# Regrouping the f32 matmuls of a two-layer trunk: transposes of a head in one run, weighted values ahead of the next scores, numerators two at a time

## The chip, the cores and the metric

The kernel runs on one core of one Trainium2 chip. The metric is the device time of one execution in microseconds (us), the median of several runs. TensorE is called PE, VectorE DVE, ScalarE ACT, SyncE SP.

## The reference, cut to what matters

The input x has 512 tokens (S) of 2048 features. It goes through two layers, each with a normalisation in front, a modulation by a conditioning vector c, a gated branch and a normalised residual.

The first layer is an mLSTM with 8 heads. In the kernel's form each head has a 512 x 512 lower-triangular weight matrix over tokens (score of key and query, times exponential gate weights), and the numerator is this matrix applied to the values:

```
s = einsum(q, k) * w_intra
num = w_inter * (q C) + s v        # 512 value columns a head
h = num / max(|den|, exp(-m))
y = sigmoid(o) * rmsnorm(h) * silu(z)
```

The second layer is attention with 16 heads of 128 features, a bias by clipped distance, and chunks of 64 tokens; with 512 tokens all earlier chunks are in reach:

```
s = einsum(q, k) * scale + bias
p = softmax(s)
o = p v                            # 128 columns a head
y = o * silu(z)
```

## The kernel before, in words

Everything is float32. A large matmul is not done in plain f32: both operands are split into a high and a low part of the type fp32r (helper `split`, L181: a cast on ACT, L182, and a subtraction on DVE, L183), and three matmuls add up high x high, high x low and low x high (`mm3`, L226, through `mm`, L223 and L224). Such a triple is the unit of most of the work. Some small matmuls stay in plain f32: one call of `mm` on f32 tiles, which PE runs as two instructions, and the transposes of L1070, one instruction each.

Weights come from memory in pieces of up to 128 x 1024 (`wpiece`, L188), in one fixed order, through SP's DMA queue (L200). Each piece is split into high and low (tiles wh and wl); for projections by a seven-product scheme (`proj_s`, L266) sums of weight blocks (ws, L207 to L209) are made on DVE and split as well (wsh, wsl).

PSUM has eight banks, one tile of 128 x 512 f32 each. Five belong to projections (`newp`, psP), three to all else (`newa`, psA). A scheduler orders each engine's instructions by data dependence, by the order in the program and by priorities; `tc.high_priority(AHEAD)` lets evacuations go first. A tile of a pool of n buffers waits until the tile n places earlier has been read.

mLSTM, one pass of the loop at L632 per head: the projections q, k; the values (ps_v) with the score tiles woven in (`scores`, L601); the gates o and z; the sum of weights ps_d; then the numerators, L732 to L744. For each of four column tiles i of the head's values, ps_n takes nine fp32r matmuls (j = 0, 1, 2: 512, 384 and 256 columns, the weights being triangular) and one f32 matmul of 128 columns (L737). ACT squares it (L740), DVE multiplies it into the gate (L741) and adds up the squares (L744). ps_q sums these over partitions (L746).

Attention, the loop at L1097: pass h projects queries and gate of head h (`queries`, L1026, one `proj_s` of four pieces). Between its pieces stand the steps of the two heads before, given as a table {1: turn, 2: mid, 3: end}. A head's life is: `weights` (L1045) for row tiles 0 and 3 in mid, and for 1 and 2 in end, of the pass after its projection: scores ps_s, with tile 0 in f32 (kt and zq) and the others by triples; the bias and the maximum in one DVE instruction (L1058), the exponential on ACT (L1059), the reciprocal and the multiplication by it on DVE (L1060, L1061). Then `flipped` (L1064) transposes the 128 x 128 blocks of the row tiles (triangular: ten of them) into ps_t and splits them into pt: column tiles 0 and 1 at the end of the pass (L1126), tiles 2 and 3 in turn (L1101). Each column tile has a bank of its own. Finally `mixed` (L1086) in mid multiplies by the values: ps_o, nine fp32r matmuls and one f32 (vt), then the gate (L1093) and a store (y2c, L1094). In mid the scores of head h-1 stand ahead of the weighted values of head h-2, and the fetch of the next k (`fetch_k`, kt, L1016) stands behind both.

Behind the attention the last projection (b_w_out, ps_y) reads y2c; the attention's last steps are woven into its first matmuls.

Of the kernel before, what the change touches and what calls it, by code (L numbers as in the profile page):

```python
# [9 lines left out]
F32 = mybir.dt.float32  # L10
F32R = mybir.dt.float32r
AF = mybir.ActivationFunctionType
ALU = mybir.AluOpType
AX = mybir.AxisListType

P = 128
D = 2048
S = 512
KT = D // P
NH = 8  # L20
# [7 lines left out]
BH = 16  # L28
# [4 lines left out]
AHEAD = 300  # L33
# [93 lines left out]
GHEAD = CBIAS + 32  # L127
# [5 lines left out]
def hybrid_trunk(ctx, tc, xT, xN, c, adaT, cols, wst, wg, ext, kc, out):  # L133
    nc = tc.nc
# [8 lines left out]
    def pool(name, bufs=1, **kw):  # L143
        return tc.tile_pool(name=name, bufs=bufs, reuse_waits="tile", **kw)
# [31 lines left out]
    def col(i):  # L176
        return cl[:, i : i + 1]
# [3 lines left out]
    def split(hi, lo, src):  # L181
        nc.scalar.copy(hi, src)  # L182
        nc.vector.tensor_tensor(lo, src, hi.bitcast(F32), op=ALU.subtract)  # L183
# [39 lines left out]
    def mm(ps, a, b, start, stop):  # L223
        nc.tensor.matmul(ps, a, b, start=start, stop=stop)  # L224

    def mm3(ps, ah, al, bh, bl, start, stop):  # L226
        mm(ps, ah, bh, start, False)
        mm(ps, ah, bl, False, False)
        mm(ps, al, bh, False, stop)
# [121 lines left out]
    def newp(name):  # L351
        return psP.tile([P, S], F32, tag="p", name=name)

    def newa(name):
        return psA.tile([P, S], F32, tag="a", name=name)
# [8 lines left out]
    tp = phA.enter_context(pool("t1", bufs=3, side="right"))  # L364
# [42 lines left out]
    for q in range(4):  # L407
        t = sp.tile([P, 4, S], F32, name=f"xt{q}")
# [8 lines left out]
    for i in range(4):  # L417
        ps = newp(f"ps_c{i}")
# [3 lines left out]
    pss = newa("ps_x")  # L422
# [5 lines left out]
    for q in range(4):  # L428
        pair = []
        for i in range(2):  # L430
            sq = xp.tile([P, 2, S], F32, tag="x", name=f"xsq{q}_{i}")
# [28 lines left out]
    for k0, k1 in BLOCKS:  # L460
# [10 lines left out]
        for i, acc in enumerate(later):  # L471
            ps = newa(f"ps_l{i}_{k0}")
# [128 lines left out]
    def scores(h, j, qk, pr, nm, nmd, tot):  # L601

        n = S - P * j
        t0 = min(P * j, 256)
        ps = newa(f"ps_s{h}_{j}")
        for kk in range(2):
            q, k = qk[kk], qk[2 + kk]
            s = slice(j * P, (j + 1) * P)
            mm3(ps[:, : S - t0], k[:, 0, s], k[:, 1, s], q[:, 0, t0:], q[:, 1, t0:], kk == 0, kk == 1)
        psn = ps[:, P * j - t0 : S - t0]  # L610
        e = tp.tile([P, S], F32, tag="t", name=f"e{h}_{j}")
        a = aT[:, j, h : h + 1]
        nc.scalar.activation(e[:, 0:P], nmd[:, j, :], AF.Exp, bias=a)
        if n > P:
            nc.scalar.activation(e[:, P:n], nm[:, P * (j + 1) :], AF.Exp, bias=a)
        if j < 3:
            with tc.high_priority(AHEAD):
                nc.vector.scalar_tensor_tensor(e[:, :n], psn, DK**-0.5, e[:, :n], op0=ALU.mult, op1=ALU.mult)
            t = hp.tile([P, 2, n], F32R, tag=f"p{j}", name=f"p{h}_{j}")
            split(t[:, 0, :], t[:, 1, :], e[:, :n])  # L620
        else:
            t = hp.tile([P, n], F32, tag=f"p{j}", name=f"p{h}_{j}")
            nc.vector.scalar_tensor_tensor(t, psn, DK**-0.5, e[:, :n], op0=ALU.mult, op1=ALU.mult)
        pr.append(t)
        if j == 0:
            tot.append(e)
        else:
            nc.vector.tensor_tensor(
                tot[0][:, P * j :], tot[0][:, P * j :], e[:, :n] if j < 3 else t, op=ALU.add
            )  # L630

    for h in range(NH):  # L632
# [3 lines left out]
        if h == 0:  # L636
            so = oz[:4]
        qk = []
        for i in range(4):
            if h > HALF:  # L640
                if i % 2 == 0:
                    zs = pair((i // 2) * (V0 // 2) + h * DK, f"zq{h}_{i}")
                ps = zs[i % 2]
            elif h < 2:
                ps = (lead, qk1)[h][i]
            else:
                ps = newp(f"ps_qk{h}_{i}")
# [24 lines left out]
        pr, tot = [], []  # L672
        at = {8 + 2 * j: lambda j=j: scores(h, j, qk, pr, nm, nmd, tot) for j in range(4)} if h else {}
# [10 lines left out]
        v = []  # L684
        for m in range(4):
            with tc.high_priority(AHEAD):
                if m < 3:
                    t = hp.tile([P, 2, S], F32R, tag="qk", name=f"v{h}_{m}", bufs=4)
                    split(t[:, 0, :], t[:, 1, :], pv[m])
                else:  # L690
                    t = hp.tile([P, S], F32, tag="nm", name=f"v{h}_{m}")
# [4 lines left out]
        if h:  # L696
            so = []
        for i in range(4):
            if h >= HALF:
                f = HEAD_PAIRS if h > HALF else RAMP[i]  # L700
# [5 lines left out]
            elif h:  # L706
                ps = newp(f"ps_o{h}_{i}")
# [4 lines left out]
        for i in range(4):  # L712
            if h >= HALF:
                break
            if h:
                ps = newp(f"ps_z{h}_{i}")
                proj_a("a_w_in", h1, ps)
            else:
                ps = oz[4 + i]
# [9 lines left out]
        nc.vector.tensor_tensor(dd, dd, em, op=ALU.max)  # L729
        nc.scalar.activation(dd, dd, AF.Square, scale=EPS**0.5)  # L730
        sqs = hp.tile([P, S], F32, tag="nmd", name=f"sqs{h}")
        for i in range(4):  # L732
            d = slice(i * P, (i + 1) * P)
            ps = newa(f"ps_n{h}_{i}")
            for j in range(3):
                mm3(ps[:, P * j :], v[j][:, 0, d], v[j][:, 1, d], pr[j][:, 0, :], pr[j][:, 1, :], j == 0, False)
            mm(ps[:, 384:], v[3][:, d], pr[3], False, True)  # L737
            with tc.high_priority(AHEAD):
                sq = sqs if i == 0 else tp.tile([P, S], F32, tag="t", name=f"sq{h}_{i}")
                nc.scalar.activation(sq, ps, AF.Square)  # L740
                nc.vector.scalar_tensor_tensor(so[i], ps, col(GHEAD + 4 * h + i), so[i], op0=ALU.mult, op1=ALU.mult)  # L741
            if i:
                with tc.high_priority(AHEAD if h == NH - 1 else 0):
                    nc.vector.tensor_tensor(sqs, sqs, sq, op=ALU.add)  # L744
        ps = newa(f"ps_q{h}")
        sums(ps, sqs, f"q{h}", *((AHEAD, 80) if h == NH - 1 else ()))  # L746
        nc.vector.scalar_tensor_tensor(dd, ps, 1.0 / DV, dd, op0=ALU.mult, op1=ALU.add)
# [19 lines left out]
    tp = tst.enter_context(pool("t2", bufs=6, side="right"))  # L767
# [127 lines left out]
    def scale_steps(*ks):  # L895
        at = {k: lambda: (scale_sums(), scale_load()) for k in ks}
        return at | {k + 2: scale_load for k in ks}
# [3 lines left out]
    for pair, ms in enumerate(PAIRS):  # L901
        for g in range(1, 4):
            at = scale_steps(4, 12, 20, *([28] if g < 3 else [])) if pair == 0 else {}
            if pair == 0 and g == 3:
                at[28] = lambda: (scale_sums(), amul_cols(2, 48 + KT, GPRE + KT))
            if pair == 1 and g == 1:
                at = {2: lambda: residual(0), 4: lambda: residual(1)}
                at |= {20 + 4 * i: lambda i=i: turned(0, [i], False) for i in range(3)}
            if pair == 1 and g == 2:
                at = {2: lambda: turned(0, [3], False)}  # L910
            if pair == 1 and g == 3:
                at = {k: lambda k=k: [key_input(i, kept(i, slice(0, 2 * P)), slice(0, 2 * P)) for i in range(k // 2 - 1, k // 2 + 1)] for k in range(2, 32, 4)}
# [60 lines left out]
    for i in range(KT // 2):  # L973
        z = zp.tile([P, 4, 256], F32, tag="z", name=f"zk{i}")
        ready = len(hs)
        at = {2: input_sums} if ready < KT // 2 else {}
# [8 lines left out]
    for g in range(2, 4):  # L985
        n = -(-ATT_PAIRS // 2)
# [22 lines left out]
    at = ast.enter_context(pool("att"))  # L1009
# [51 lines left out]
            nc.vector.tensor_scalar(s, s, r, None, op0=ALU.mult)  # L1061
            pr[i] = s

    def flipped(h, pr, js):  # L1064
        pts = []
        for j in js:
            n = S - P * j
            ps = newa(f"ps_t{h}_{j}")
            for i in range(j, 4):
                nc.tensor.transpose(ps[:, P * (i - j) : P * (i - j + 1)], pr[i][:, P * j : P * (j + 1)], ident)  # L1070
            with tc.high_priority(AHEAD):
                if j < 3:
                    t = at.tile([P, 2, n], F32R, tag=f"pt{j}", name=f"pt{h}_{j}")
                    split(t[:, 0, :], t[:, 1, :], ps[:, :n])
                else:
                    t = at.tile([P, n], F32, tag=f"pt{j}", name=f"pt{h}_{j}")
                    nc.scalar.copy(t, ps[:, :n])
            pts.append(t)
        return pts

# [5 lines left out]
    def mixed(h, pts, v, sz):  # L1086
        ps = newa(f"ps_o{h}")
        for j in range(3):
            d = slice(P * j, P * (j + 1))
            mm3(ps[:, P * j :], v[:, 0, d], v[:, 1, d], pts[j][:, 0, :], pts[j][:, 1, :], j == 0, False)  # L1090
        mm(ps[:, 384:], vt[h][:, 384:], pts[3], False, True)
        with tc.high_priority(AHEAD):
            nc.vector.tensor_tensor(sz, ps, sz, op=ALU.mult)  # L1093
        nc.sync.dma_start(y2c[h // 2][:, h % 2, :], sz)  # L1094

    qs, pts, prs, vs, szs = {}, {}, {}, {}, {}
    for h in range(BH + 2):  # L1097

        def turn():
            if h > 1:  # L1100
                pts[h - 2] += flipped(h - 2, prs.pop(h - 2), (2, 3))  # L1101
                vs[h - 2] = split_v(h - 2)

        def mid():
            if 0 < h <= BH:
                weights(h - 1, (0, 3), *qs[h - 1])
            if h > 1:
                mixed(h - 2, pts.pop(h - 2), vs.pop(h - 2), szs.pop(h - 2))
            if 0 < h < BH:
                fetch_k(h)  # L1110
            if h < BH:
                fetch_v(h)

        def end():
            if 0 < h <= BH:
                weights(h - 1, (1, 2), *qs[h - 1])
                prs[h - 1] = qs.pop(h - 1)[0]

        if h < BH:
            qs[h], szs[h] = queries(h, {1: turn, 2: mid, 3: end})  # L1120
        else:
            turn()
            mid()
            end()
        if 0 < h <= BH:
            pts[h - 1] = flipped(h - 1, prs[h - 1], (0, 1))  # L1126
    ast.close()


# [1 line left out]
    op = ost.enter_context(pool("op", bufs=KT))  # L1131
# [64 lines left out]
    for g in range(4):  # L1196
        if g:
            spare[0] = rp
        for pair in [range(4)] if g < 3 else PAIRS:
            ps = [newp(f"ps_y1_{g}_{m}") for m in pair]  # L1200
            at = {4: lambda: finish(0), 6: lambda: finish(1)} if pair == PAIRS[1] else {}
# [65 lines left out]
```

## Time and profile before

| | |
|---|---|
| median of 3 runs | 2799.73 us (2799.65 to 2801.61) |
| profiled execution | 2801.9 us |
| its span, first to last instruction | 2800.1 us |
| granted TensorE clock, mean | 0.998 |
| DMA | 527.09 MB, mean 188 GB/s |
| transposes ps_t | 160, median record 272 ns |
| f32 block of ps_o (vt) | 32 instructions, median record 275 ns |

A row of the timeline has the start in us, the length, the engine, the line, the operation and its tiles (output, then inputs), the shape, and the number of equal instructions merged; matmuls are pipelined, so the lengths of neighbours overlap, and the distance between starts is what PE spends. A row of the windows view has the stretch, its length, and the busy time of PE, weight loads (PEld), DVE, ACT and GpSimd with their instruction counts, then the granted clock, the DMA share and GB/s. A row of the waits view has who waited for whom, the sum in us, how often, and the longest.

### The profile page before, as it was taken

What the parts mean: (1) busy time and instruction counts of PE and PEld (TensorE: products, weight loads), DVE (VectorE), ACT (ScalarE), POOL (GpSimd) and SP (SyncE); (2) the same over time, 40 slices, a digit from 0 to 9 for tenths busy, and PEclk for the clock granted to TensorE, in tenths of its full rate; (3) what the DMA queues carried; (4) which work ended last, traced back from release to release, by engine and by line L of the source; (5) the groups of instructions that cost most, each with busy time, mean ns of one, the idle gap of its engine ahead of it and who ended that gap; (6) DMA issues with size and microseconds to landing.
All of it is one profiled execution on the core that took longest, in us unless ns stands there. A gap on an engine that the chain in (4) does not pass through costs nothing.

```text
span 2800.1 us, 42223 instructions
## 1 busy us (share of the span) xinstructions
PE 2767.4 (99%) x15959; PEld 2440.4 (87%) x15959; DVE 2157.3 (77%) x3788; ACT 1370.5 (49%) x2032; POOL 0.2 (0%) x4
## 2 busy tenths in 40 slices
PE   7999999999999999999999999999999999999998
PEld 5887888888998989989999788888999899999887
DVE  7986979769786876867867677567986788989667
ACT  4234524234454554545545344568534466666523
POOL 0000000000000000000000000000000000000000
PEclk9999999999999999999999999999999999999999
DMA  8875697865232332323324889879535544444687
GB/s 296 305 255 180 219 320 249 305 215 180 93 112 94 102 113 91 113 91 106 115 89 140 274 294 303 264 255 298 177 136 174 173 128 125 123 129 128 218 299 250
DMA packets 182999, 527.09 MB, mean 188 GB/s; under 512 B 19669, under 2 KB 38133, under 8 KB 182153
## 3 DMA queue, kind: packets, MB, share of 16 engines
q1 hardware_dynamic: 182794, 524.38, 56.6%
q8 instruction: 125, 2.05, 0.3%
q14 instruction: 80, 0.66, 0.1%
HBM read 490.69 MB, written 38.85 MB: 189 GB/s over the span
## 4 chain that ended last, share of the span: by engine, by line
PE 85%; DVE 6%; DMA 5%; issue 2%; ACT 2%; SPq 0%; DVEq 0%; ACTq 0%
PE ps_y L224 15%; PE ps_v L224 12%; PE ps_azo L224 5%; PE ps_kv L224 4%; PE ps_o L224 4%; PE ps_bzo L224 3%; PE ps_az L224 3%; PE ps_cz L224 3%; PE ps_dz L224 3%; PE ps_qk L224 3%; PE ps_z L224 3%; PE ps_czo L224 3%; PE ps_dzo L224 3%; PE ps_s L224 2%; PE ps_n L224 2%
## 5 line engine op out<-in xcount | busy, mean ns | idle before, releaser
L182 ACT CAST wh<-wr 128x1024 fp32r<-128x1024 f32 (+3 forms) x586 | 585.3, 1000 | 707.4 <-PE ps_y L224 151.8
L183 DVE TENSOR_TENSOR wl<-wr,wh 128x1024 fp32r<-128x1024 f32 (+3 forms) x586 | 679.1, 1161 | 284.6 <-ACT wh L182 283.5
L224 PE MATMUL ps_y<-wh,y 128*128 128x512 f32 x1536 | 478.1, 391 | 2.4 <-ACT y L182 1.8
L224 PEld LDWEIGHTS ps_y<-wh,y 128*128 128x128 f32 x1536 | 288.1, 188 | 64.8 <-ACT y L182 3.0
L182 ACT CAST wsh<-ws 128x384 fp32r<-128x384 f32 (+1 forms) x261 | 163.3, 626 | 361.0 <-PE ps_az L224 126.1
L224 PE MATMUL ps_v<-wh,h 128*128 128x512 f32 x1024 | 322.7, 391 | 0.4 <-DVE zq L318 0.4
L224 PE MATMUL ps_y<-wl,y 128*128 128x512 f32 x768 | 299.5, 390 | 0.0
L183 DVE TENSOR_TENSOR wsl<-ws,wsh 128x384 fp32r<-128x384 f32 (+1 forms) x261 | 181.8, 697 | 121.2 <-ACT wsh L182 119.4
L224 PEld LDWEIGHTS ps_v<-wh,h 128*128 128x128 f32 x1024 | 192.5, 188 | 40.9 <-DVE zq L318 0.9
L224 PE MATMUL ps_v<-wl,h 128*128 128x512 f32 x512 | 199.8, 390 | 0.0
L224 PEld LDWEIGHTS ps_y<-wl,y 128*128 128x128 f32 x768 | 144.3, 188 | 29.5 <-DVE wl L183 0.3
L224 PE MATMUL ps_kv<-wh,hkv 128*128 128x512 f32 x512 | 159.4, 391 | 0.0
L207 DVE TENSOR_TENSOR ws<-wr 128x256 f32<-128x256 f32 (+1 forms) x261 | 132.2, 516 | 33.4 <-DMA wr<-in_wst 31.3
L382 DVE CUSTOM_DVE_ANT_0 ada<-ada,scB,mod 128x1024 f32<-128x1024 f32 x96 | 123.0, 1282 | 16.4 <-DMA ada<-in_adaT 15.4
L382 DVE CUSTOM_DVE_ANT_0 ada<-ada,scB,cl 128x1024 f32<-128x1024 f32 x96 | 122.9, 1281 | 13.0 <-DMA ada<-in_adaT 12.8
L224 PEld LDWEIGHTS ps_kv<-wh,hkv 128*128 128x128 f32 x512 | 96.2, 188 | 19.7
L224 PEld LDWEIGHTS ps_v<-wl,h 128*128 128x128 f32 x512 | 96.3, 188 | 19.5 <-issue 0.9
L224 PE MATMUL ps_azo<-h,wh 128*128 128x256 f32 (+1 forms) x406 | 101.4, 332 | 1.1 <-DVE zo L318 1.1
L224 PE MATMUL ps_l<-h,wh 128*128 128x512 f32 x320 | 99.4, 393 | 0.5 <-ACT oz L475 0.5
L224 PE MATMUL ps_kv<-wl,hkv 128*128 128x512 f32 x256 | 99.9, 390 | 0.0
L224 PE MATMUL ps_czo<-h1s,wsh 128*128 128x256 f32 x468 | 89.3, 283 | 0.0
L209 DVE TENSOR_TENSOR ws<-wr 128x128 f32<-128x128 f32 (+1 forms) x261 | 85.2, 336 | 3.6
(390 smaller groups left out, 6266.0 us busy)
## 6 DMA issues: line engine op xcount, KB each, us to landing
wr<-in_wst SPq DMA_DIRECT2D x520, 512.0 KB, 3.7
ada<-in_adaT SPq DMA_DIRECT2D x224, 512.0 KB, 6.0
adq<-in_adaT SPq DMA_DIRECT2D x64, 256.0 KB, 5.7
xt<-nsc SPq DMA_DIRECT2D x48, 256.0 KB, 4.0
yr<-ysc SPq DMA_DIRECT2D x16, 512.0 KB, 4.6
wr<-in_wst SPq DMA_DIRECT2D x30, 256.0 KB
wr<-in_wst SPq DMA_DIRECT2D x16, 384.0 KB, 9.6
bsc<-in_ext SPq DMA_DIRECT2D x16, 320.0 KB, 6.5
```

Source lines behind the costliest of these rows:

```text
L182: nc.scalar.copy(hi, src)
L183: nc.vector.tensor_tensor(lo, src, hi.bitcast(F32), op=ALU.subtract)
L207: nc.vector.tensor_tensor(t[:, : 2 * w], r[:, w : 3 * w], r[:, : 2 * w], op=ALU.subtract)
L209: nc.vector.tensor_tensor(t[:, 2 * w :], r[:, 3 * w :], r[:, w : 2 * w], op=ALU.subtract)
L224: nc.tensor.matmul(ps, a, b, start=start, stop=stop)
L382: pin(nc.vector.tensor_tensor_reduce(at, at, (sc or scB)[:, j * D // 2 : (j + 1) * D // 2], 1.0, mod[:, i : i + 1] if j else col(CB + i), ...
```

## The change

Three edits. In the mLSTM the numerators are written in twos: the nine fp32r matmuls of both tiles first, then both f32 matmuls, then both evacuations. In the attention all ten transposes of a head are done in turn, one after the other, into three banks (column tile 3 shares the bank of tile 1); the call at the end of the pass is gone. In mid the weighted values of head h-2 stand ahead of the scores of head h-1.

```diff
-        for i in range(4):
-            d = slice(i * P, (i + 1) * P)
-            ps = newa(f"ps_n{h}_{i}")
-            for j in range(3):
-                mm3(ps[:, P * j :], v[j][:, 0, d], v[j][:, 1, d], pr[j][:, 0, :], pr[j][:, 1, :], j == 0, False)
-            mm(ps[:, 384:], v[3][:, d], pr[3], False, True)
...
+        for i0 in (0, 2):
+            pss = [newa(f"ps_n{h}_{i}") for i in (i0, i0 + 1)]
+            ds = [slice(i * P, (i + 1) * P) for i in (i0, i0 + 1)]
+            for ps, d in zip(pss, ds):
+                for j in range(3):
+                    mm3(ps[:, P * j :], v[j][:, 0, d], v[j][:, 1, d], pr[j][:, 0, :], pr[j][:, 1, :], j == 0, False)
+            for ps, d in zip(pss, ds):
+                mm(ps[:, 384:], v[3][:, d], pr[3], False, True)
+            for i, ps in zip((i0, i0 + 1), pss):
...
-    def flipped(h, pr, js):
-        pts = []
-        for j in js:
-            n = S - P * j
-            ps = newa(f"ps_t{h}_{j}")
+    def flipped(h, pr):
+
+        banks = [newa(f"ps_t{h}_{j}") for j in range(3)]
+        pss = [banks[0], banks[1][:, :384], banks[2][:, :256], banks[1][:, 384:]]
+        for j, ps in enumerate(pss):
             for i in range(j, 4):
                 nc.tensor.transpose(ps[:, P * (i - j) : P * (i - j + 1)], pr[i][:, P * j : P * (j + 1)], ident)
+        pts = []
+        for j, ps in enumerate(pss):
             with tc.high_priority(AHEAD):
...
         def turn():
             if h > 1:
-                pts[h - 2] += flipped(h - 2, prs.pop(h - 2), (2, 3))
+                pts[h - 2] = flipped(h - 2, prs.pop(h - 2))
                 vs[h - 2] = split_v(h - 2)
 
         def mid():
+            if h > 1:
+                mixed(h - 2, pts.pop(h - 2), vs.pop(h - 2), szs.pop(h - 2))
             if 0 < h <= BH:
                 weights(h - 1, (0, 3), *qs[h - 1])
-            if h > 1:
-                mixed(h - 2, pts.pop(h - 2), vs.pop(h - 2), szs.pop(h - 2))
...
-        if 0 < h <= BH:
-            pts[h - 1] = flipped(h - 1, prs[h - 1], (0, 1))
```

More of the change, by code (lines that the diff above doesn't have):

```diff
@@ L731, in hybrid_trunk @@
         sqs = hp.tile([P, S], F32, tag="nmd", name=f"sqs{h}")
-        for i in range(4):
-            d = slice(i * P, (i + 1) * P)
-            ps = newa(f"ps_n{h}_{i}")
-            for j in range(3):
-                mm3(ps[:, P * j :], v[j][:, 0, d], v[j][:, 1, d], pr[j][:, 0, :], pr[j][:, 1, :], j == 0, False)
-            mm(ps[:, 384:], v[3][:, d], pr[3], False, True)
[L738 to L744, printed above, removed]
+        for i0 in (0, 2):
[7 more added lines that the diff above has]
+            for i, ps in zip((i0, i0 + 1), pss):
+                with tc.high_priority(AHEAD):
+                    sq = sqs if i == 0 else tp.tile([P, S], F32, tag="t", name=f"sq{h}_{i}")
+                    nc.scalar.activation(sq, ps, AF.Square)
+                    nc.vector.scalar_tensor_tensor(so[i], ps, col(GHEAD + 4 * h + i), so[i], op0=ALU.mult, op1=ALU.mult)
+                if i:
+                    with tc.high_priority(AHEAD if h == NH - 1 else 0):
+                        nc.vector.tensor_tensor(sqs, sqs, sq, op=ALU.add)
         ps = newa(f"ps_q{h}")
@@ L1062, in weights @@
             pr[i] = s
-    def flipped(h, pr, js):
-        pts = []
-        for j in js:
-            n = S - P * j
-            ps = newa(f"ps_t{h}_{j}")
+    def flipped(h, pr):
+        banks = [newa(f"ps_t{h}_{j}") for j in range(3)]
+        pss = [banks[0], banks[1][:, :384], banks[2][:, :256], banks[1][:, 384:]]
+        for j, ps in enumerate(pss):
             for i in range(j, 4):
                 nc.tensor.transpose(ps[:, P * (i - j) : P * (i - j + 1)], pr[i][:, P * j : P * (j + 1)], ident)
+        pts = []
+        for j, ps in enumerate(pss):
             with tc.high_priority(AHEAD):
                 if j < 3:
-                    t = at.tile([P, 2, n], F32R, tag=f"pt{j}", name=f"pt{h}_{j}")
-                    split(t[:, 0, :], t[:, 1, :], ps[:, :n])
-                else:
-                    t = at.tile([P, n], F32, tag=f"pt{j}", name=f"pt{h}_{j}")
-                    nc.scalar.copy(t, ps[:, :n])
+                    t = at.tile([P, 2, S - P * j], F32R, tag=f"pt{j}", name=f"pt{h}_{j}")
+                    split(t[:, 0, :], t[:, 1, :], ps)
+                else:
+                    t = at.tile([P, P], F32, tag=f"pt{j}", name=f"pt{h}_{j}")
+                    nc.scalar.copy(t, ps)
             pts.append(t)
```

## The prediction

> **What bounds the kernel now.** I read the page first: which engine is busy, and which engine the chain that ended last runs through.
>
> ```profile
> span 2800.1 us, 42223 instructions
> PE 2767.4 (99%) x15959; PEld 2440.4 (87%) x15959; DVE 2157.3 (77%) x3788; ACT 1370.5 (49%) x2032; POOL 0.2 (0%) x4
> PE 85%; DVE 6%; DMA 5%; issue 2%; ACT 2%; SPq 0%; DVEq 0%; ACTq 0%
> ```
>
> TensorE (PE) is busy for 99% of the span, so I asked next for its busy time in the stretches that the edits touch: the numerators of one head (1509 to 1532 us, the last of eight), the attention (2255 to 2628), and four microseconds of its end.
>
> ```profile
> 1509.00:1532.00 23.00, 23.00 (x118) 19.85 (x117) 17.73 (x27) 14.63 (x22) 0.00 (x0) 1.00 0.54 176
> 2255.00:2628.00 373.00, 372.85 (x2949) 365.55 (x2949) 333.93 (x734) 245.74 (x434) 0.00 (x0) 1.00 0.45 139
> 2622.00:2626.00 4.00, 4.00 (x25) 3.29 (x23) 2.48 (x5) 2.89 (x7) 0.00 (x0) 1.00 0.98 374
> ```
>
> The columns after the stretch are its length, then PE, weight loads, DVE and ACT. PE stands still for 0.15 us of 373 in the attention and not at all in the numerators; the clock is 1.00. The waits of PE, for 284 to 1532 us and for 2255 to 2640 us, have these as their longest:
>
> ```profile
> PE ps_azo L224 <- DVE zo L318: 1.1, 1, 1.1
> PE ps_t L1070 <- DVE pt L183: 0.2, 1, 0.2
> ```
>
> So no wait is there to be removed: an edit gains only if PE needs less time for the same matmuls, and it loses where PE begins to wait. That decides the method: what does PE pay at the borders that the change removes?
>
> **Part 1, the borders.** The program's matmuls come in two kinds: the triples of L224 on fp32r operands, and plain f32 ones: the transposes of L1070, the first score tile (kt, zq), the last block of ps_o (vt), and the 128-column matmul of L737. Counted in the instruction order of the two programs, PE meets 140 separate runs of f32 before and 57 after: 83 fewer. The matmuls themselves are the same, 160 transposes included. In the timeline of PE a row's second column overlaps its neighbours, so I use distances from start to start. First a lone transpose, then runs of two and four.
>
> ```profile
> 2259.14 0.40 PE L224 MATMUL ps_bz<-h2s,wh 128*128 128x256 f32 x2
> 2259.50 0.27 PE L1070 MATMUL ps_t<-kcs,s 128*128 128x128 f32 x1
> 2259.53 0.48 PE L224 MATMUL ps_dz<-h2s,wh 128*128 128x256 f32 x2
> 2259.97 0.40 PE L224 MATMUL ps_dz<-h2s,wh 128*128 128x256 f32 x2
> ```
>
> ```profile
> 2263.92 0.38 PE L1070 MATMUL ps_t<-kcs,s 128*128 128x128 f32 x2
> 2264.06 0.48 PE L224 MATMUL ps_bz<-h2s,wh 128*128 128x256 f32 x2
> 2264.49 0.28 PE L224 MATMUL ps_bz<-h2s,wh 128*128 128x256 f32 x1
> 2264.61 0.60 PE L1070 MATMUL ps_t<-kcs,s 128*128 128x128 f32 x4
> 2264.97 0.36 PE L224 MATMUL ps_bz<-h2s,wh 128*128 128x256 f32 x1
> 2265.17 0.28 PE L224 MATMUL ps_bz<-h2s,wl 128*128 128x256 f32 x1
> 2265.29 0.38 PE L1070 MATMUL ps_t<-kcs,s 128*128 128x128 f32 x2
> ```
>
> A triple alone takes 2259.50 - 2259.14 = 0.36 us. One transpose and a triple take 2259.97 - 2259.50 = 0.47, so the transpose costs 0.11. Two and a triple take 2264.49 - 2263.92 = 0.57, so 0.21 for two. Four and a triple take 2265.29 - 2264.49 = 0.80, so 0.44 for four. The end of the attention has a run of six between 512-column triples:
>
> ```profile
> 2619.37 0.62 PE L224 MATMUL ps_y<-wh,y 128*128 128x512 f32 x2
> 2620.05 0.62 PE L224 MATMUL ps_y<-wh,y 128*128 128x512 f32 x2
> 2621.65 0.82 PE L1070 MATMUL ps_t<-kcs,s 128*128 128x128 f32 x6
> 2623.01 0.63 PE L224 MATMUL ps_y<-wh,y 128*128 128x512 f32 x2
> ```
>
> There a triple takes 0.68, and 2623.01 - 2621.65 = 1.36, so 0.68 for six. Runs of 1, 2, 4 and 6 cost 0.11, 0.21, 0.44 and 0.68: 0.11 apiece and nothing per run. The first fp32r matmul behind a run shows 0.48 where 0.40 is usual, which looks like a price of leaving f32. But it began only 0.03 us after the transpose: 0.03 + 0.08 is the transpose's own 0.11.
>
> The ten transposes of a head now cost 0.11 + 0.21 + 0.44 + 0.21 + 0.11 = 1.08; in one run 1.10. Over 16 heads that is +0.3 us, which is rounding.
>
> **Part 2, weighted values ahead of scores.** The last f32 block of ps_o now meets the f32 score tile.
>
> ```profile
> 2295.45 0.39 PE L224 MATMUL ps_s<-kt,zq 128*128 128x128 f32 x2
> 2296.38 1.73 PE L224 MATMUL ps_o<-pt,vv 128*128 128x512 f32 x9
> 2297.95 0.39 PE L224 MATMUL ps_o<-pt,vt 128*128 128x128 f32 x2
> 2298.09 0.49 PE L224 MATMUL ps_dz<-h2s,wh 128*128 128x256 f32 x2
> ```
>
> A matmul of this kind is two instructions. From 2295.45 to 2296.38 is 0.93, of which three 512-column matmuls are 0.68 (above), so 0.25 for the pair; two pairs in one run would take 4 x 0.11 = 0.44 in place of 0.50. That is -0.06 a head at most, -1.0 us over 16, and nothing by the transposes' own law. I take half, -0.5 us.
>
> What is queued behind: ps_o stands 0.93 us earlier, the scores 1.71 us later (2296.38 to 2298.09, the ten instructions now ahead of them). Their softmax has until the transposes of the next head; only its second half, tiles 1 and 2, which stays where it is, is late there (the rival below). On SP the fetch of the next kt (L1016) is now issued behind the store of the weighted values (L1094), where it was ahead:
>
> ```profile
> 2295.87 0.33 SPq L1016 DMA_DIRECT2D kt<-ksc  x1
> 2299.26 0.38 SPq L1094 DMA_DIRECT2D y2c<-z  x1
> ```
>
> ```profile
> 2304.31 0.62 ACT L182 CAST k<-kt 128x512 fp32r<-128x512 f32 x1
> ```
>
> ```profile
> kt<-ksc SPq DMA_DIRECT2D x16, 256.0 KB, 3.1
> ```
>
> Issued at about 2299.7 and landing 3.1 us later (2302.8), kt still meets its cast at 2304.31 with 1.5 us to spare. Cost nothing; if that cover went, ACT would stand still for the excess and PE would first notice through the weight casts behind it.
>
> **Part 3, three banks at once and the evacuation.** The ten transposes take all three banks of psA, and tile 1 shares one with tile 3, so its evacuation waits for the last transpose. In the changed order of DVE the weights' low part (L183, wl) also stands ahead of the three evacuations.
>
> ```profile
> 2290.56 1.48 DVE L183 TENSOR_TENSOR pt<-ps_t,pt 128x512 fp32r<-128x512 f32 x3
> 2292.07 1.23 DVE L183 TENSOR_TENSOR wl<-wr,wh 128x1024 fp32r<-128x1024 f32 x1
> ```
>
> Swapped, the evacuation ends at 2290.56 + 1.23 + 1.48 = 2293.3. ps_o would now start at 2295.45, so 2.1 us cover it, and it costs nothing. Each us beyond that would cost PE 16 us in all.
>
> **Part 4, numerators by twos.** In the changed order only tiles 0 and 1 of each head join their f32 ends (in the first head tiles 2 and 3 too): 9 joins at the 0.00 to 0.06 of part 2, so -0.5 to 0; I take -0.2 us. Tile 3 needs the bank of tile 0. Between tile 0's end and tile 3's start PE now has tile 1's f32 pair (0.25), tile 2 (1.57 as in ps_o, whose widths are the same, plus 0.25) and a triple (0.36): 2.4 us. Releasing the bank took, in the fourth head,
>
> ```profile
> 790.21 0.60 ACT L740 ACTIVATE sqs<-ps_n 128x512 f32<-128x512 f32 x1 [1.21 <-PE ps_n L224]
> 790.87 0.74 DVE L741 SCALAR_TENSOR_TENSOR zo<-ps_n,cl,zo 128x512 f32<-128x512 f32 x1
> ```
>
> 790.21 to 791.61 = 1.4 us. That leaves 1.0 us, less than the 1.23 of one wl that might stand ahead on DVE: at worst 0.2 us in each of eight heads, +1.8 us. I take 0.
>
> **The sum.** +0.3 - 0.5 - 0.2 = -0.4 us on a span of 2800.1. The profiled execution took 2801.9 us (1.8 around its span), the three runs 2799.65 to 2801.61 with a median of 2799.73. Against that median the forecast is 2799.3 us. Such a step can't be told from no change; about 0.2%, 5.6 us, can.
>
> **The rivals.**
>
> *A, a price per border.* If the 0.08 us by which the first record behind a run is longer were a stall of its own, 83 borders would give 83 x 0.08 = 6.6 us, so 2793.1. For it speaks only that record; against it, that the cost per transpose is the same for one as for six. The Trainium skill, "TensorEngine Tiling (Array Packing)", Key Properties, says that a change of tiling mode drains TensorE. By that rule, if the element kind counted as such a mode, A would hold; every row above says 128*128 whatever the kind, and the trace shows no drain. Chance 5%.
>
> *B, the one run waits for softmax, and the kernel is slower.* The third transpose reads score tile 2, and that is ready late:
>
> ```profile
> 2313.52 0.41 DVE L1061 TENSOR_SCALAR s<-s,mx 128x384 f32<-128x384 f32 x1
> ```
>
> ```profile
> 2314.91 0.38 PE L1070 MATMUL ps_t<-kcs,s 128*128 128x128 f32 x2
> ```
>
> The tile is ready at 2313.93. All triples of that piece end at 2314.91, with 0.11 + 0.21 + 0.44 of transposes ahead, so the joined run would start at 2314.15 and its third member at 2314.37: 0.44 us to spare. From there each delay on DVE is PE's, since all ten stand in order with no triple between. If one wl (1.23 us) moved ahead of L1061, PE would wait 0.8 us in 16 heads: +12.8 us, 2812. Against it: DVE's order between the scores and this point is as before, and DVE is busy for 333.93 of the attention's 373 us only. With the smaller waits of part 4 and of the attention's end, chance 6%.
>
> *C, the clock.* If the clock gate took a run of 1.1 us for idleness and halved the clock for as long, 16 x 1.1 us would be added, 2817. Against it: the stretch with the run of six has 1.00. The Trainium skill, "TensorE: Matmul & The Clock Gate", Part 4, says that transposes don't count as busy for the gate; this trace, with that run and a clock of 1.00, shows no effect. Chance 1%.
>
> **How the numbers follow.** The forecast, no change within 0.2%, has 88%, A 5%, B and C 7%. Within it the bounds are -1.0 - 0.5 = -1.5 us, with the two waits quoted first (1.1 and 0.2) going as well -2.8, and +0.3 + 1.8 = +2.1 us; the runs themselves reach 1.9 above their median. That makes 2796.9 to 2803.7, which holds a little over 8 in 10.
>
> **What would show it.** After the change, the distance from the first of ten transposes to the second triple behind them should be 1.1 us more than a triple (A would show less); ps_s behind ps_o 0.44 for its four f32 instructions and PE's idle time in the attention below 1 us. A wait of ps_t for L1061, or of ps_n for L741, of more than 0.3 us a head would be B; a clock below 1.00, C. I am wrong if the time moves more than 5.6 us.

## The result and the profile after

| | before | after |
|---|---|---|
| median, us (range, runs) | 2801.64 (2798.34 to 2805.93, 20) | 2806.03 (2801.62 to 2809.88, 20) |
| ratio to before, with its 95% interval | | 1.0014 [1.0008, 1.002] |
| profiled execution's span, us | 2800.1 | 2804.8 |

The change makes the kernel slower by 4.4 us, with the interval 2.2 to 5.6. The forecast was no change within 0.2%, and it is within 0.2%. But the sign is the other one (-0.4 was forecast), and 2806.03 lies outside the range of 2796.9 to 2803.7. Of the 6.7 us between forecast and result, 1.9 are the level of before itself: three runs had given 2799.73, twenty give 2801.64. The other 4.8 are the 4.4 of the change and the 0.4 that was forecast to be gained.

The page of after, its span and engines:

```profile
span 2804.8 us, 42216 instructions
PE 2768.6 (99%) x15959; PEld 2441.4 (87%) x15959; DVE 2158.5 (77%) x3788; ACT 1372.6 (49%) x2032; POOL 0.2 (0%) x4
```

PE is busy for 2768.6 us where it was 2767.4, with the same 15959 matmuls: the work costs what it did, and the loss is time in which PE stands still. The windows view of after, for the numerators and the attention:

```profile
1509.00:1532.00 23.00, 21.44 (x113) 18.42 (x112) 16.86 (x27) 15.04 (x23) 0.00 (x0) 1.00 0.47 156
2255.00:2628.00 373.00, 371.54 (x2947) 364.44 (x2946) 334.19 (x733) 246.96 (x429) 0.00 (x0) 1.00 0.44 136
```

In the attention PE now stands still for 373.00 - 371.54 = 1.46 us, where it was 0.15; in the last head's numerators for 1.56, where it was nothing. The clock is 1.00 in both. The waits of PE in after's attention (2255 to 2640 us), then what ACT and DVE wait for there and in before never did:

```profile
PE ps_t L1073 <- DVE s L1064: 0.9, 3, 0.3
PE ps_o L224 <- DVE pt L183: 0.5, 1, 0.5
```

```profile
ACT k L182 <- DMA kt<-ksc: 1.8, 2, 1.0
DVE z L315 <- ACT zq L314: 2.0, 3, 1.0
```

(L1073 and L1064 are before's L1070 and L1061, three lines further down.) The transposes wait for the softmax multiplication, which is the place that rival B named. ACT waits for kt, and DVE for a copy on ACT by which a projection's bank is emptied (zq<-ps_dz, L314). The tile view of kt in after has the time from issue to landing:

```profile
DMA to landing us min/median/max: 6.2/6.2/6.2
```

It was 3.1. Least, median and most are one number because the profile has the landing of one transfer of the sixteen only (of before it has two); the starts of the casts, below, tell of all. One head of after shows the way from kt to PE. First SP's issues, then ACT:

```profile
2276.11 0.36 SPq L200 DMA_DIRECT2D wr<-in_wst  x1
2276.71 0.33 SPq L1099 DMA_DIRECT2D y2c<-z  x1
2277.15 0.36 SPq L1019 DMA_DIRECT2D kt<-ksc  x1
```

```profile
2281.85 1.04 ACT L182 CAST wh<-wr 128x1024 fp32r<-128x1024 f32 x1
2283.86 0.62 ACT L182 CAST k<-kt 128x512 fp32r<-128x512 f32 x1 [0.96 <-DMA kt<-ksc]
2284.89 0.60 ACT L1062 ACTIVATE s<-s,mx 128x384 f32<-128x384 f32 x1
2285.49 0.35 ACT L314 COPY zq<-ps_dz 128x256 f32<-128x256 f32 x1
```

SP issues a weight piece, the store and kt within 1.4 us. ACT is free for the cast of k at 2281.85 + 1.04 = 2282.89, which is 5.7 us behind kt's issue; the cast begins at 2283.86, 6.7 us behind it. Behind that cast in ACT's order stand the exponentials of tiles 1 and 2 of the other head and the copy of ps_dz. They need nothing of kt, and are late by as much. Then DVE and PE in the same head:

```profile
2285.87 0.42 DVE L315 TENSOR_TENSOR z<-zq,ps_dz 128x256 f32<-128x256 f32 x1 [0.98 <-ACT zq L314]
2293.07 0.41 DVE L1064 TENSOR_SCALAR s<-s,mx 128x384 f32<-128x384 f32 x1
```

```profile
2292.37 0.27 PE L1073 MATMUL ps_t<-kcs,s 128*128 128x128 f32 x1
2292.88 0.33 PE L1073 MATMUL ps_t<-kcs,s 128*128 128x128 f32 x1 [0.23 <-DVE s L1064]
2293.54 1.09 PE L1073 MATMUL ps_t<-kcs,s 128*128 128x128 f32 x8 [0.34 <-DVE s L1064]
2294.39 0.48 PE L224 MATMUL ps_dz<-h2s,wh 128*128 128x256 f32 x2
```

The exponential itself is not what comes late to PE: it ends at 2284.89 + 0.60 = 2285.49, and its tile is multiplied only at 2293.07. The copy is what counts. DVE waits 0.98 us for it, and then works through its order without a wait: 7.20 us from L315 to the multiplication, here as in the next head, in which kt came in time (2310.52 to 2317.72). So the multiplication is as late as the copy. The score tile is finished at 2293.07 + 0.41 = 2293.48, and the last eight transposes start at 2293.54. From the first transpose to the triple behind all ten it is 2294.39 - 2292.37 = 2.02 us; the next head has all ten in one row and takes 2319.20 - 2318.19 = 1.01 (rows below). The late kt costs PE 1.01 us in this head, more than the 0.23 + 0.34 that the waits view counts. So the place is clear; whether kt makes the time is for the experiments, since the numerators changed too.

### The profile page after: what moved, and what is told of

It is laid out like the page before. It is cut to its first block, busy times and chain, and to the rows that moved or that the text cites. A ratio compares the mean times of both kernels' runs of the same rounds, so it can differ in the third digit from the quotient of the medians.

```text
span 2804.8 us, 42216 instructions
## 1 busy us (share of the span) xinstructions
PE 2768.6 (99%) x15959; PEld 2441.4 (87%) x15959; DVE 2158.5 (77%) x3788; ACT 1372.6 (49%) x2032; POOL 0.2 (0%) x4
## 4 chain that ended last, share of the span: by engine, by line
PE 85%; DVE 6%; DMA 5%; issue 2%; ACT 2%; SPq 0%; DVEq 0%; ACTq 0%
PE ps_y L224 15%; PE ps_v L224 11%; PE ps_azo L224 5%; PE ps_kv L224 4%; PE ps_o L224 4%; PE ps_bzo L224 3%; PE ps_qk L224 3%; PE ps_z L224 3%; PE ps_cz L224 3%; PE ps_az L224 3%; PE ps_dz L224 3%; PE ps_czo L224 3%; PE ps_dzo L224 3%; PE ps_s L224 2%; PE ps_azq L224 2%
```

## The experiments

Each was timed beside before. Median, ratio with its 95% interval, and from each profile's attention: how long behind kt's issue ACT is free for the cast of k (median of the 13 full passes), how long behind it that cast begins (least to most), and PE's waits of ps_t for the softmax (us in how many waits):

| kernel | median, us | ratio to before | ACT free | cast begins | ps_t waits |
|---|---|---|---|---|---|
| before | 2800.6 to 2801.6 | | 8.5 | 8.4 | none |
| after | 2806.03 | 1.0014 [1.0008, 1.002] | 5.5 | 5.2 to 6.7 | 0.9 in 3 |
| after, repeated | 2805.56 | 1.0016 [1.0008, 1.0025] | 5.5 | 5.4 to 6.7 | 0.8 in 3 |
| numerators alone | 2801.80 | 0.9999 [0.9989, 1.0009] | 8.5 | 8.4 | none |
| both attention edits | 2804.42 | 1.0009 [1.0001, 1.0018] | 5.5 | 5.4 to 6.7 | 1.4 in 5 |
| ten transposes alone | 2801.25 | 1.0001 [0.9992, 1.001] | 8.5 | 8.4 | none |
| weighted values first, alone | 2804.68 | 1.0012 [1.0004, 1.0021] | 5.5 | 5.4 to 6.5 | 2.6 in 4 |
| after, kt's fetch ahead again | 2802.71 | 1.0004 [0.9995, 1.0013] | 10.0 | 9.9 | none |
| weighted values first, kt ahead | 2801.25 | 1.0001 [0.9992, 1.0009] | 9.9 | 9.8 | none |
| before, kt's fetch behind the store | 2815.97 | 1.0053 [1.004, 1.0066] | 4.7 | 3.7 to 7.2 | 13.1 in 13 |

(Neighbouring instructions overlap by 0.1 us on ACT, so a cast that waits for nothing begins 0.1 ahead of the column before. A head can have two waits: the three of each profile of after stand in two heads, the five of both attention edits in three.) Where ACT is free 8.5 us or more behind the issue, the cast always begins at once, to 0.01 us. Where it is free at 5.5 or 4.7, the cast's start scatters.

### Which of the edits: four kernels with parts of the change

**The numerators alone.** The diff's block of the numerators, the attention as before.

> Only the numerators by twos; the attention as before (131 f32 runs on PE in place of 140). Theory W (waits): the 4.4 us come from new waits of PE at the changed places, and the numerators' part is the wait of ps_n in the last head (1.6 us in the one profile of the changed kernel) and the later scores of the second head: +1 to +2.5 us, with a wait of ps_n for L744 in the profile again. Theory N (nothing): the part is 0 within 1 us, since the next projection (ps_y) stands on waits for ACT that swallow what came late before it.

Measured 0.9999 [0.9989, 1.0009]: no price and no gain to be seen. Yet its trace has a new wait, the largest of PE in the last head (1509 to 1620 us), first this kernel, then after, then before:

```profile
PE ps_n L224 <- DVE zo L744: 1.3, 1, 1.3
PE ps_y L224 <- ACT y L182: 0.3, 1, 0.3
```

```profile
PE ps_n L224 <- DVE zo L744: 1.6, 1, 1.6
PE ps_y L224 <- ACT y L182: 1.3, 1, 1.3
```

```profile
PE ps_y L224 <- ACT y L182: 1.8, 3, 0.8
PE ps_y L224 <- ACT sqy L799: 0.6, 1, 0.6
```

The new wait takes the place of part of an old one: the projection behind it (ps_y) used to wait 1.8 + 0.6 us for ACT and now waits 0.3. The sums differ from one profile to the next: 0.6 to 2.4 us in the six with before's numerators (mean 1.7), 1.6 to 3.8 in the four with the new ones (mean 3.0). That hints at 1.3 us, less than the times of this kernel can tell: their interval goes from 3.1 us of gain to 2.5 of loss.

**Both attention edits, the numerators as before.**

> Both attention edits without the numerators (66 f32 runs in place of 140). Theory W: the rest of the 4.4 us, +2 to +3.5 us, and it is seen as waits of ps_t for L1064 or ps_o for pt in the profile. Theory B- (borders cost less than nothing: a weight load in reserve behind each): +0.2 us, without waits. Theory D (drift): the 4.4 us are mostly timing of DMA in stages that the change doesn't touch; then this kernel is within 1 us of before.

Measured 1.0009 [1.0001, 1.0018], with ACT's waits for kt, DVE's for L314 (3.3 us) and PE's for the softmax as in after. The loss is in the attention.

**The ten transposes in one run, alone.** The mid step as before, so kt's fetch is where it was.

```diff
-                pts[h - 2] += flipped(h - 2, prs.pop(h - 2), (2, 3))
+                pts[h - 2] = flipped(h - 2, prs.pop(h - 2))
...
-        if 0 < h <= BH:
-            pts[h - 1] = flipped(h - 1, prs[h - 1], (0, 1))
```

> Only the ten transposes in one run, scores still ahead of the weighted values (82 f32 runs). Theory W: waits of ps_t for the softmax's last multiplication and the attention's end: +1 to +3 us. Theory B-: +0.2 us.

Measured 1.0001 [0.9992, 1.001], with no wait of ps_t at all. PE meets 82 runs of f32 here where before has 140. A price per border would have shown: at rival A's 0.08 us it is 4.6 us, and the interval ends at 2.2 us of gain.

**Weighted values ahead of the scores, alone.**

```diff
         def mid():
-            if 0 < h <= BH:
-                weights(h - 1, (0, 3), *qs[h - 1])
             if h > 1:
                 mixed(h - 2, pts.pop(h - 2), vs.pop(h - 2), szs.pop(h - 2))
+            if 0 < h <= BH:
+                weights(h - 1, (0, 3), *qs[h - 1])
```

> Only the weighted values ahead of the next scores, transposes as before (124 f32 runs). Theory W: if the later scores make softmax late, waits of ps_t here too and +1 to +2 us; if the one run of transposes makes the waits, 0 within 1 us. Theory B-: 0.

Measured 1.0012 [1.0004, 1.0021]: the whole loss again, from this edit alone. Its waits of PE and of ACT in the attention:

```profile
PE ps_t L1070 <- DVE s L1061: 2.6, 4, 0.8
```

```profile
ACT k L182 <- DMA kt<-ksc: 3.7, 4, 1.0
```

This edit moves two things: the matmuls on PE, and on SP the store that now goes ahead of kt's fetch. The next kernels take them apart.

### Which part of that edit: the order on PE or the order on SP

**After, with kt's fetch ahead again.** The fetch can't simply be put first: the f32 score of the head before still reads the old kt tile. So the 128 columns that this score needs are copied to a tile of their own (16 more copies on ACT), and the fetch goes to the top of mid. PE's order is after's.

```diff
+        k0 = at.tile([P, P], F32, tag="k0", name=f"k0_{h}")
+        nc.scalar.copy(k0, kt[h][:, :P])
...
-                mm(ps[:, :n], q0, kt[h][:, :P], True, True)
+                mm(ps[:, :n], q0, k0, True, True)
...
         def mid():
+            if 0 < h < BH:
+                fetch_k(h)
...
-            if 0 < h < BH:
-                fetch_k(h)
```

> The changed kernel, with the 128 columns of kt that the f32 score tile reads copied on ACT (16 copies more), so that kt's one buffer is free before the scores and its fetch is issued ahead of the store of the weighted values, as before the change; the order on DVE is the changed kernel's, line for line. Theory K (the fetch of kt): the waits of ACT for the DMA of kt and those of ps_t for L1064 go, and the time falls by 2 to 4.5 us to within 1.5 us of before. Theory S (the later scores themselves make softmax late): the waits of ps_t stay and so does the time, +4 us over before.

Its DMA view:

```profile
kt<-ksc SPq DMA_DIRECT2D x16, 256.0 KB, 2.7
```

kt lands in 2.7 us (two transfers of the sixteen), ACT doesn't wait for it, DVE not for L314 and PE for nothing in the attention, and the time is 1.0004 [0.9995, 1.0013]. Beside after, repeated on the same chip, it is 2805.56 - 2802.71 = 2.9 us faster (1.4 to 4.6 when the runs of both are resampled), with all the change's matmul order in place.

**Weighted values first alone, with the same edit.**

> Weighted values ahead of the scores alone, with the same copy and early fetch. Theory K: from the 4.1 us of that edit alone to 0 within 1.5 us, no wait of ACT for kt, no wait of ps_t for L1061 (there were four, 0.4 to 0.75 us each). Theory S: as without the copy, +4 us.

Measured 1.0001 [0.9992, 1.0009], against 1.0012 without the edit. Here ACT does wait for kt, but at another instruction:

```profile
ACT k L1039 <- DMA kt<-ksc: 5.7, 7, 2.0
```

L1039 is the new copy, which ACT reaches well ahead of the cast. DVE never waits for L314 here (without this edit 3.8 us, in four heads), and the multiplication is never late: PE's one wait, 0.9 us, is for an evacuation. A wait by itself costs nothing; it depends on what stands behind it. These waits also show how long kt takes ahead of the store, with a weight piece issued 1.2 us before it: of the 13 full passes, seven have the copy wait, and start it 3.4 to 5.2 us behind the issue; in the other six kt was there by 3.4.

**Before, with only SP's order changed.** The reverse: no matmul moves, and the store of y2c and the fetch of kt are held in the order of the program, which puts kt behind the store.

```diff
-        nc.sync.dma_start(ts[h], src)
+        ins = nc.sync.dma_start(ts[h], src)
+        if tag == "kt":
+            pin(ins)
...
-        nc.sync.dma_start(y2c[h // 2][:, h % 2, :], sz)
+        pin(nc.sync.dma_start(y2c[h // 2][:, h % 2, :], sz))
```

> The kernel before, with nothing changed but the place of kt's fetch on SP: behind the store of the weighted values, as the change has it; the orders on PE, DVE and ACT are those of before, line for line. The store is about 0.9 us later here than in the changed kernel. Theory K: ACT waits for kt and PE for L1061, in more heads than after the change: +4 us or more. Theory S: within 1 us of before.

Measured 1.0053 [1.004, 1.0066], +15 us, with PE's, DVE's and ACT's instructions in before's order. The attention in its windows view, its waits of PE, ACT and DVE, and one head of it on SP and on ACT:

```profile
2255.00:2628.00 373.00, 359.39 (x2844) 351.39 (x2843) 318.52 (x697) 236.22 (x405) 0.00 (x0) 1.00 0.40 126
```

```profile
PE ps_t L1072 <- DVE s L1063: 13.1, 13, 2.3
```

```profile
ACT k L182 <- DMA kt<-ksc: 16.7, 13, 2.5
DVE z L315 <- ACT zq L314: 16.9, 13, 2.5
```

```profile
2297.55 0.38 SPq L1096 DMA_DIRECT2D y2c<-z  x1
2297.98 0.42 SPq L1016 DMA_DIRECT2D kt<-ksc  x1
```

```profile
2301.65 1.05 ACT L182 CAST wh<-wr 128x1024 fp32r<-128x1024 f32 x1
2303.64 0.62 ACT L182 CAST k<-kt 128x512 fp32r<-128x512 f32 x1 [0.93 <-DMA kt<-ksc]
```

ACT is free for the cast at 2302.70, 4.7 us behind the issue, and the cast begins at 2303.64, 5.7 behind it. Since ACT waits in nearly every pass here, the starts of the casts are kt's own time: 5.4 to 7.2 us, in the median 5.7 (in one pass kt is issued 3 us behind the store, and takes 3.7). So one order on SP makes the same chain of waits, in the same places, and larger.

**After once more,** to see how much of the first profile is the change.

> The changed kernel once more, on the same chip as these: for the comparison, and for what its profile shows a second time. +3 to +5.5 us over before; waits of ACT for kt in some heads and of ps_t for L1064 behind them; the stages of K and V (1880 to 2217 us), whose orders on all engines the change leaves alone, differ from the first profile by 1 us or more if they are a matter of DMA timing.

Measured 1.0016 [1.0008, 1.0025]. Its waits of ACT and of PE in the attention:

```profile
ACT k L182 <- DMA kt<-ksc: 2.1, 3, 1.1
```

```profile
PE ps_t L1073 <- DVE s L1064: 0.8, 3, 0.3
```

The wait comes back, in three heads instead of two. In after kt comes just when it is due: ACT is free 5.5 us behind the issue, and kt's own time is 5.4 to 5.8 in most heads and 6.3 to 7.2 in a few (above; one head of after had it in 5.2 or less). So most heads lose nothing or 0.2 us, and two of each profile 0.8 to 1.1 us on ACT. Another head of after, of the first kind, on SP and on ACT:

```profile
2302.53 0.33 SPq L1099 DMA_DIRECT2D y2c<-z  x1
2302.95 0.38 SPq L1019 DMA_DIRECT2D kt<-ksc  x1
```

```profile
2307.39 1.05 ACT L182 CAST wh<-wr 128x1024 fp32r<-128x1024 f32 x1
2308.51 0.63 ACT L182 CAST k<-kt 128x512 fp32r<-128x512 f32 x1
```

ACT is free at 2308.44, 5.5 us behind the issue, and begins at 2308.51. The two profiles of after also differ by 3.4 us between the last ps_x and the last ps_kv (301.3 and 297.9 us; 298.3 in before), where all engines have before's order. In the first of them the granted clock is 0.50 there from 1992 to 1995 us, behind two waits of PE for DVE (1.27 and 0.69 us); in the second and in before it stays at 1.00. So that part of a single profile isn't put down to the change.

## Why the prediction was right and wrong

**The step that failed** is the last of Part 2: "Issued at about 2299.7 and landing 3.1 us later (2302.8), kt still meets its cast at 2304.31 with 1.5 us to spare. Cost nothing". The move was seen, the queue and the neighbour named, and then kt was given the landing time of its old place. Behind the store it takes 5.4 to 7.2 us, in the median 5.7. Before's own DMA view had a row to warn of it, that of the transfer which kt was to follow:

```profile
y2c<-z SPq DMA_DIRECT2D x16, 256.0 KB, 5.3
```

At 5.3 us the forecast's 2299.7 gives 2305.0, 0.7 us late for the cast at 2304.31, and not 1.5 early. There was a second slip, in the other direction: the store goes with ps_o, which the prediction itself put 0.93 us earlier. That makes the issue 2298.8 and leaves 5.5 us to the cast, which is what the runs show. So the step had two bounds, 3.1 and 5.3, and a cover of 5.5 that the upper one all but used up: not "cost nothing" but a wait in some heads.

**What followed a late kt** was also too mild. The prediction had PE notice "first through the weight casts behind it". What DVE notices first is the copy of ps_dz behind the cast, and what PE notices, 7.20 us of DVE's work later, is the multiplication: the place of rival B. B had the place right, and looked for the cause on DVE alone, as a wl moved ahead. Its slack, 0.44 us by the rows of before, is 0.28 in after's head in time (tile ready at 2317.72 + 0.41 = 2318.13, third transpose at 2318.19 + 0.22 = 2318.41). The order of DVE did stay as it was; the delay came in on ACT, from a queue two engines away. Rival B's 2812 was a wait of 0.8 us in 16 heads; in after two heads lose 1.0 and 0.6 us. Those two heads show the sign that the prediction gave for B, more than 0.3 us; and PE's idle time in the attention, 1.46 us, is above the 1 us that the forecast allowed.

**The size.** On one chip, after is 4.6 us above before, and 2.9 of these go when kt's fetch is put ahead again. What is left (1.0004, between 1.4 us of gain and 3.6 of loss) can't be told from nothing; the 1.3 us that the profiles hint at in the last head's numerators would fit it, but are not shown. The profiles agree with the 2.9: from the first ps_az to the last ps_y they have 573.0 and 572.8 us for after and 569.9 with kt's fetch ahead (571.4 for before). Of that difference the two late heads are 1.6 and 1.8 us, by the distance from the first transpose to the triple behind all ten. The rest, 1.5 and 1.1 us, lies at the attention's end (ps_o) and behind it, where ps_gg waits for a gate (1.0 and 1.4 us in after, 0.5 with kt ahead). That last wait is 1.7 us in before, where kt is in time; so how much of the rest is kt's isn't shown.

**Part 1 was right.** Ten transposes in after, and the next two triples:

```profile
2318.19 1.25 PE L1073 MATMUL ps_t<-kcs,s 128*128 128x128 f32 x10
2319.20 0.48 PE L224 MATMUL ps_dz<-h2s,wh 128*128 128x256 f32 x2
...
2319.64 0.40 PE L224 MATMUL ps_dz<-h2s,wh 128*128 128x256 f32 x2
```

2319.64 - 2318.19 = 1.45, less a triple of 0.36 is 1.09 for ten: 0.11 apiece, as in runs of one to six. Rival A is out, by this and by the kernel with the ten transposes alone. The Trainium skill's rule of a drain at a change of tiling mode ("TensorEngine Tiling (Array Packing)", Key Properties) therefore doesn't speak of a change between fp32r and f32.

**Part 2's matmuls were right.** The f32 pairs of ps_o and ps_s now meet:

```profile
2325.89 0.39 PE L224 MATMUL ps_o<-pt,vt 128*128 128x128 f32 x2
2326.11 0.39 PE L224 MATMUL ps_s<-kt,zq 128*128 128x128 f32 x2
2326.25 0.94 PE L224 MATMUL ps_s<-k,q 128*128 128x512 f32 x3
2327.03 0.40 PE L224 MATMUL ps_dz<-h2s,wh 128*128 128x256 f32 x2
```

2327.03 - 2325.89 = 1.14, less 0.68 for three 512-column matmuls is 0.46 for four f32 instructions; 0.44 was forecast by the one law and 0.50 by the other. The kernel with weighted values first and kt ahead is at 1.0001, so the gain of 0.5 us is too small to be seen, if it is there.

**Part 3 held** within the heads: ps_o waits for the evacuation once, 0.5 us, at the attention's end. **Part 4 held** as far as the times can tell (0.9999), though not in its detail: in the last head ps_n waits for its bank 1.3 to 1.6 us where 0.2 was the worst case, and the projection behind it, which waited there before, gets only part of that back. **Rival C** is out: in after's attention every stretch of 20 us has a clock of 1.00.

**The level.** A median of three runs was taken as before's time to 0.1 us; twenty runs put it 1.9 us higher, within a spread of 2798.34 to 2805.93. The range had allowed 1.9 us for the runs, and used all of it for that.

## What to carry to other kernels

When an edit moves a fetch past another transfer on its queue, price its landing from the row of the transfer that it will follow, not from its own old row, and set that against the time from issue to first use. Then read what stands behind the waiting instruction on its engine, work of other heads included, and who waits for that: here the delay went from the cast on ACT to a copy behind it, from there to DVE, and over 7.20 us of DVE's queue to PE. So an engine that is idle half of the time can still hold one that is busy for 99%.

## What the runs showed of the hardware that was not expected

**How long a 256 KB fetch takes from issue to landing goes here with what was issued just ahead of it on its queue.** With a 512 KB weight piece 2.6 us ahead it took 2.7 to 3.3 us (the two landings each of before and of after with kt ahead). With the piece 1.2 us ahead, in the kernel with weighted values first and kt ahead, it took up to 5.2 us. With the piece 0.9 us and a 256 KB store 0.4 us ahead it took 5.4 to 7.2 us (the casts that waited for it in the kernel before with kt's fetch behind the store). The first head hints at the store as the larger part: there a weight piece stands 0.4 us ahead and no store within 3 us, and kt took 3.9 to 4.4 us in the eight profiles in which the cast waited for it. But the traffic around it is another there, and no run moved the store alone.

**PE at half its clock after short waits.** Before's windows around the longest early wait of PE, and the row in it:

```profile
62.00:68.00 6.00, 3.43 (x16) 2.49 (x14) 5.86 (x11) 1.45 (x2) 0.00 (x0) 0.95 1.00 401
68.20:73.40 5.20, 5.20 (x12) 4.10 (x13) 5.13 (x9) 1.35 (x2) 0.00 (x0) 0.50 0.98 346
```

```profile
68.15 2.50 PE L224 MATMUL ps_lead<-h,wh 128*128 128x512 f32 x5 [2.72 <-ACT h L359]
```

Behind a wait of 2.72 us the granted clock is 0.50 for over 5 us, though PE then works without a pause. The Trainium skill, "TensorE: Matmul & The Clock Gate", Part 1, puts the idle window that halves the clock, and the busy one that restores it, at about 3.4 us each. The kind of effect agrees; here 2.72 us in one piece, with PE busy for 3.43 of 6 us, was enough. So was less: in that kernel with kt's fetch behind the store, PE waits 1.90 us for the softmax, until 2598.83, and two windows behind that wait have these rows:

```profile
2600.00:2603.00 3.00, 3.00 (x17) 3.00 (x15) 2.67 (x5) 2.28 (x4) 0.00 (x0) 0.50 0.03 10
2604.00:2607.00 3.00, 3.00 (x27) 3.00 (x26) 0.34 (x1) 0.48 (x1) 0.00 (x0) 1.00 0.54 175
```

The row of 373 us above rounds this away to 1.00. The twelve other waits of that kernel for the softmax, up to 2.3 us, left the clock at 1.00; so the length of the wait alone doesn't decide it here. Ask for the clock in windows as short as the effect.
